# One recurrence stage, four engines: squares and weight halves change engine, and a GELU polynomial is written in one operation fewer

## The chip, the core and the metric

The kernel runs on one core of one Trainium2 chip, in one launch. Its engines are TensorE (PE, matrix products), VectorE (DVE), ScalarE (ACT), GpSimd (POOL) and SyncE (SP, which issues all the DMAs here). Each engine takes its own instructions in order, and semaphores order them against each other. The metric is the device time of the launch in microseconds (us), as the median of several runs.

## The reference, cut to what matters

The program is one layer of an encoder on a 1024 x 1024 float32 input: a mixer, and then a gated feed-forward network with a convolution. Half of the mixer is a gated linear recurrence over the sequence in both directions, the other half attention. The change lies in the recurrence, and in one weight load of the attention that falls into the same stretch of time.

```python
r = sigmoid(xh @ w_a + b_a);  i = sigmoid(xh @ w_x + b_x)      # the gates, block by block
log_a = -LRU_C * r * softplus(-lam)
a = exp(log_a)
u = sqrt(-expm1(2.0 * log_a)) * (i * xf)                        # scaled input of the recurrence
h = associative_scan(a * h_before + u)                          # one forward, one backward
y_lru = gelu(lru_g) * (h_forward + h_backward)
```

The GELU is the one with tanh: 0.5 p (1 + tanh(GK (p + 0.044715 p^3))).

## The kernel before, in words

Channels lie on the 128 partitions and the sequence of 1024 positions on the free axis. Products are made with three float32r matmuls each: an operand is split into an upper half (a rounded copy) and a lower half (the rest), by `split(hi, lo, src, hi_on, lo_on)` at L60 to L67. The upper half is a copy on ACT (L62), DVE (L64) or POOL (L66); the lower half is a subtraction on DVE or POOL (both L67).

The recurrence has 512 channels, so four blocks j = 0 to 3 of 128 channels. For each block and both directions d: a gate product on PE (`psg`), its tanh on ACT (L487), the decay `a` by Exp on ACT (L203), its square (`square_a`, L210, on POOL), a second function of the same gate by Tanh on ACT (L207), their product on DVE (`decay_mul`, L213), one square root for both directions (`root`, L216, on ACT, with a table load in front of it), the gated input (L490, DVE), its scaling (`scale_in`, L219: direction 0 on DVE, direction 1 on POOL), the scan (L223, DVE), the sum of the directions (L226), and the product with the GELU (L229). The GELU of block j is `gelu_a` (L232 to L234) and `gelu_b` (L237 and L238): a square on ACT, a multiply-add and a product on DVE, a tanh on ACT, a last step on DVE that is also the last reader of the PSUM tile `psG`. PSUM has three large tiles in this stretch, for `psg`, `psG` and `psx` (the input projection of a later block) in turn.

Weights come as float32 by DMA into staging tiles `st` (three of them) and are split into tiles `w` (three of them) or `gwt` (gate weights, one): `load` in the block loop, `load_gates` and `load_kv`. Upper halves of these are on DVE, lower halves on POOL.

Two ways of ordering meet here. In blocks 0 and 1 only PE has an order written by hand; the other engines' instructions are put in order when the program is built, by a planner with its own estimates of time. From `xc3 = conv_a(3)` on (blocks 2 and 3, up to the start of the attention loop) the order in the source is the order on PE, ACT, DVE and POOL. The attention loop after it (t = 2 to 60) is again by hand on PE alone.

Of the kernel before, what the change touches and what calls it, by code (L numbers as in the profile page):

```python
# [12 lines left out]
AF = mybir.ActivationFunctionType  # L13
ALU = mybir.AluOpType
# [3 lines left out]
P = 128  # L18
# [22 lines left out]
def encoder_layer(ctx, tc, x, w_in, wq, wk, wv, gw, wo, wup, wdn, vec, g_mix, g_ffn, g_fin, g_q, g_kv, tab_t, tab_n, out):  # L41
    nc = tc.nc
    act, dve, pool, pe = nc.scalar, nc.vector, nc.gpsimd, nc.tensor
# [16 lines left out]
    def split(hi, lo, src, hi_on="act", lo_on="dve"):  # L60
        if hi_on == "act":
            act.activation(hi, src, AF.Copy)  # L62
        elif hi_on == "dve":
            dve.tensor_copy(hi, src)  # L64
        else:
            pool.tensor_scalar(out=hi, in0=src, scalar1=1.0, scalar2=1.0, op0=ALU.mult, op1=ALU.mult)  # L66
        (dve if lo_on == "dve" else pool).tensor_tensor(out=lo, in0=src, in1=hi.bitcast(F32), op=ALU.subtract)  # L67

    def mm3(ps, l, r, start, stop):
        pe.matmul(ps, l[0], r[0], start=start, stop=False)  # L70
        pe.matmul(ps, l[0], r[1], start=False, stop=False)  # L71
        pe.matmul(ps, l[1], r[0], start=False, stop=stop)  # L72
# [39 lines left out]
    def load_w(col, name, src, hi_on="act", lo_on="pool", st=None):  # L112
        if st is None:
            st = stp.tile([P, NK, P], F32, tag="st", name=name + "s")
        nc.sync.dma_start(out=st, in_=src[:, col:col + P].rearrange("(k p) n -> p k n", p=P))
        w = wp.tile([P, 2, NK, P], F32R, tag="w", name=name)
        split(w[:, 0], w[:, 1], st, hi_on, lo_on)
        return w
# [36 lines left out]
    def bigA(name):  # L155
        return psA.tile([P, 1024], F32, tag="big", bufs=3, name=name)
# [6 lines left out]
    def proj_x(j, wx):  # L163
        psx[j] = bigA(f"psx{j}")
        for hf in range(2):
            project(psx[j], wx, xT, hf)

    def proj_g(j, wg, hf, ks=range(NK)):
        if j not in psG:
            psG[j] = bigA(f"psG{j}")  # L170
        project(psG[j], wg, xT, hf, ks)
# [8 lines left out]
    attn = {}  # L180

    def load_kv():
        st = stp.tile([P, S], F32, tag="st", name="wkvst")
        nc.sync.dma_start(out=st[:, 0:512], in_=wk)
        nc.sync.dma_start(out=st[:, 512:1024], in_=wv)
        attn["kv"] = wp.tile([P, 2, S], F32R, tag="w", name="wkv")
        split(attn["kv"][:, 0], attn["kv"][:, 1], st, "dve", "pool")

    def stage_q(k):
        st = stp.tile([P, S], F32, tag="st", name=f"wqst{k}")  # L190
# [10 lines left out]
    def decay_exp(j, d, a):  # L201
        c = lru_c[:, 2 * j + d:2 * j + d + 1]
        act.activation(a, bc[:, d, :], AF.Exp, scale=c, bias=c)  # L203

    def decay_tanh(j, d):
        c = lru_c[:, 2 * j + d:2 * j + d + 1]
        act.activation(bc[:, d, :], bc[:, d, :], AF.Tanh, scale=c, bias=c)  # L207

    def square_a(a, a2):
        pool.tensor_tensor(out=a2, in0=a, in1=a, op=ALU.mult)  # L210

    def decay_mul(d, a2):
        dve.scalar_tensor_tensor(out=bc[:, d, :], in0=a2, scalar=1.0, in1=bc[:, d, :], op0=ALU.add, op1=ALU.mult)  # L213

    def root():
        act.activation(bc[:, 0:2, :], bc[:, 0:2, :], AF.Sqrt, scale=-0.0625)  # L216

    def scale_in(d, eng=None):
        (eng or (pool if d else dve)).tensor_tensor(out=bc[:, 2 + d, :], in0=bc[:, 2 + d, :], in1=bc[:, d, :], op=ALU.mult)  # L219
# [9 lines left out]
        eng.tensor_tensor(out=y_lru[:, j, :], in0=bc[:, 2, :], in1=t1, op=ALU.mult)  # L229

    def gelu_a(t1, p):
        act.activation(t1, p, AF.Square)  # L232
        dve.tensor_scalar(out=t1, in0=t1, scalar1=0.044715, scalar2=1.0, op0=ALU.mult, op1=ALU.add)
        dve.tensor_tensor(out=t1, in0=p, in1=t1, op=ALU.mult)  # L234

    def gelu_b(t1, p):
        act.activation(t1, t1, AF.Tanh, scale=GK)  # L237
# [15 lines left out]
    if True:  # L253
# [207 lines left out]
        if True:  # L461
            def conv_a(j):
                p = psx[j]
                xc = lp.tile([P, S], F32, tag=f"xc{j % 2}", name=f"xc{j}")
                cw = lambda t: vv[:, V_CW + 4 * j + t:V_CW + 4 * j + t + 1]
                act.activation(xc, p, AF.Identity, scale=cw(2), bias=vv[:, V_CB + j:V_CB + j + 1])
                dve.scalar_tensor_tensor(out=xc[:, 2:], in0=p[:, :-2], scalar=cw(0), in1=xc[:, 2:], op0=ALU.mult, op1=ALU.add)
                dve.scalar_tensor_tensor(out=xc[:, 1:], in0=p[:, :-1], scalar=cw(1), in1=xc[:, 1:], op0=ALU.mult, op1=ALU.add)
                dve.scalar_tensor_tensor(out=xc[:, :-1], in0=p[:, 1:], scalar=cw(3), in1=xc[:, :-1], op0=ALU.mult, op1=ALU.add)
                return xc  # L470

            def conv_b(j, xc):
                xch = lp.tile([P, 2, S], F32R, tag="xch", name=f"xch{j}")
                split(xch[:, 0], xch[:, 1], xc, "dve", "dve")
                return xc, xch

            def conv(j):
                return conv_b(j, conv_a(j))

            def gate(j, d, g):  # L480
                gwt, xch = got[f"g{j}"], cv[j][1]
                psg = bigA(f"psg{j}{d}{g}")
                b = 2 * d + g
                for hf in range(2):
                    mm3(psg[:, ts(hf, 512)], (gwt[:, 0, b, :], gwt[:, 1, b, :]),
                        (xch[:, 0, ts(hf, 512)], xch[:, 1, ts(hf, 512)]), True, True)
                act.activation(bc[:, 2 * g + d, :], psg, AF.Tanh, scale=0.5, bias=gb_h[:, 4 * j + b:4 * j + b + 1])  # L487

            def gated(j, d):
                dve.scalar_tensor_tensor(out=bc[:, 2 + d, :], in0=bc[:, 2 + d, :], scalar=1.0, in1=cv[j][0], op0=ALU.add, op1=ALU.mult)  # L490

            def a_tiles(j):
                return [lp2.tile([P, S], F32, tag="a", bufs=2, name=f"a{j}{d}") for d in range(2)]

            def a2_tile(j, d):
                return lp.tile([P, S], F32, tag="a2", name=f"a2{j}{d}")

            def t1_tile(j):
                return (lp2 if j % 2 else lp).tile([P, S], F32, tag="gt", name=f"t1{j}")

            def load_gates(j, gst=None):
                if gst is None:
                    gst = stp.tile([P, 4, P], F32, tag="st", name=f"gst{j}")
                    nc.sync.dma_start(out=gst, in_=gw[:, j])
                g = lp.tile([P, 2, 4, P], F32R, tag="gw", name=f"gwt{j}")
                split(g[:, 0], g[:, 1], gst, "dve", "pool")
                return g

            got = {"X1": wx1, "G0": wG0, "g0": load_gates(0, gst0)}

            def load(k, j):
                got[f"{k}{j}"] = load_gates(j) if k == "g" else load_w((0 if k == "X" else 512) + j * P, f"w{k}{j}", w_in, "dve")

            cv = {0: conv(0)}
            proj_x(1, got["X1"])
            cv[1] = conv(1)
            order.close()
            order.enter_context(tc.manual_schedule(engines=ORDER_PE))
            for j in range(2):
                load("X", j + 2)  # L520
                aa = a_tiles(j)
                gate(j, 0, 0)
                gate(j, 1, 0)
                for d in range(2):
                    a2 = a2_tile(j, d)
                    decay_exp(j, d, aa[d])
                    square_a(aa[d], a2)
                    decay_tanh(j, d)
                    decay_mul(d, a2)
                proj_g(j, got[f"G{j}"], 0)  # L530
                gate(j, 0, 1)
                gate(j, 1, 1)
                root()
                for d in range(2):
                    gated(j, d)
                    scale_in(d)
                    scan(d, aa[d])
                add_dirs(dve)
                proj_g(j, got[f"G{j}"], 1)
                t1 = t1_tile(j)  # L540
                gelu_a(t1, psG[j])
                gelu_b(t1, psG[j])
                load("g", j + 1)
                load("G", j + 1)
                proj_x(j + 2, got[f"X{j + 2}"])
                if j == 0:
                    cv[2] = conv(2)
                merge(j, t1, dve)
                squares(j, t1)
            load("G", 3)  # L550
# [6 lines left out]
    a2 = a2_tile(2, 0)  # L557
# [10 lines left out]
    a2 = a2_tile(2, 1)  # L568
# [14 lines left out]
    t1 = t1_tile(2)  # L583
# [8 lines left out]
    a2 = [y_lru[:, 3, :], a2_tile(3, 1)]  # L592
# [126 lines left out]
    with ExitStack() as apx2:  # L719
# [112 lines left out]
        for t in range(2, NS - 3):  # L832
# [15 lines left out]
            if t in (54, 56, 58, 60):  # L848
                k = (t - 54) // 2
                if k == 3:  # L850
                    wo345 = ctpool.tile([P, 3, 2, D], F32R, tag="cT", name="wo345")
                    w = wo345[:, 0]
                else:
                    w = wp.tile([P, 2, D], F32R, tag="w", name=f"wo{k}")
# [672 lines left out]
```

## Time and profile before

| | |
|---|---|
| median of 3 runs | 1225.94 us (1224.2 to 1227.89) |
| the profiled execution, time | 1227.5 us |
| its span, first to last instruction | 1225.7 us |
| PE busy | 1167.1 us, 95% of the span |
| DVE busy | 939.6 us, 77% |
| ACT busy | 641.3 us, 52% |
| POOL busy | 260.2 us, 21% |
| mean granted TensorE clock | 0.987 of full speed |

A row of the timeline gives the start of an instruction, its duration, its engine, line and operation, the tiles it writes and reads, and in brackets how long the engine sat idle in front of it and which instruction ended that. A duration runs from an instruction's start on its engine, so it includes any time for which the instruction stood there without moving. The chain of waits is the path of work that ended last, followed back from the end. A table of windows gives busy time in each stretch.

### The profile page before, as it was taken

How to read it: one execution, taken by the hardware profiler on the slowest of the kernel's cores; microseconds unless marked ns; L12 is line 12 of the kernel's file. 1: busy time of each engine (PE TensorE's matmuls, PEld its weight loads, DVE VectorE, ACT ScalarE, POOL GpSimd, SP SyncE). 2: the span in 40 equal slices, each digit the busy share in tenths (PEclk: the TensorE clock that was granted, in tenths of full speed). 3: DMA queues.
4: the chain of work that ended last, by engine and by line, in shares of the span. 5: the costliest groups of instructions: out<-in, count | busy, mean ns of one | idle time of the engine just before them, and what ended most of it. 6: DMA issues, size and time to landing. Idle time of an engine off the chain costs nothing.

```text
span 1225.7 us, 15357 instructions
## 1 busy us (share of the span) xinstructions
PE 1167.1 (95%) x5668; PEld 970.8 (79%) x5668; DVE 939.6 (77%) x1386; ACT 641.3 (52%) x1037; POOL 260.2 (21%) x146
## 2 busy tenths in 40 slices
PE   5999986999999999998899999999999999999997
PEld 5987764788888888776778888888888888888885
DVE  5788789877777765478697778787787877887866
ACT  4735565776767764343554445444444454344453
POOL 2214556621212243254010101101010100000000
PEclk8999998999999999999999999999999999999999
DMA  5311101000000133221233232322333258853333
GB/s 211 96 43 44 43 18 35 18 1 1 1 1 1 35 138 121 68 88 51 60 121 107 77 116 96 120 95 78 112 112 121 80 178 304 288 173 119 96 112 120
DMA packets 93579, 113.38 MB, mean 92 GB/s; under 512 B 5184, under 2 KB 59840, under 8 KB 93504
## 3 DMA queue, kind: packets, MB, share of 16 engines
q1 hardware_dynamic: 93504, 112.40, 27.8%
q8 instruction: 44, 0.72, 0.3%
q14 instruction: 31, 0.25, 0.1%
HBM read 82.76 MB, written 28.57 MB: 91 GB/s over the span
## 4 chain that ended last, share of the span: by engine, by line
PE 81%; DVE 12%; ACT 2%; DMA 2%; issue 2%; SPq 0%; DVEq 0%; POOL 0%; ACTq 0%
PE vl L1076 19%; PE x L1269 9%; PE y L1269 7%; PE gh L1076 5%; PE gl L1076 4%; PE pt L763 4%; PE p L1076 4%; PE av L774 3%; PE av L773 2%; PE sc L70 2%; PE sc L71 2%; PE sc L72 2%; DVE bc L223 1%; PE pso L71 1%; PE pso L72 1%
## 5 line engine op out<-in xcount | busy, mean ns | idle before, releaser
L1076 PE MATMUL vl<-T,w 128*128 128x512 f32 x792 | 195.7, 396 | 2.0 <-ACT gl L1082 1.5
L1076 PEld LDWEIGHTS vl<-T,w 128*128 128x128 f32 x792 | 148.5, 188 | 37.8 <-ACT gl L1082 1.9
L67 POOL TENSOR_TENSOR w<-rg,w 128x1024 fp32r<-128x1024 f32 x21 | 52.0, 2475 | 363.8 <-ACT w L62 227.6
L749 DVE TENSOR_REDUCE nm<-sc 128x1 f32<-128x1024 f32 x64 | 78.1, 1221 | 29.9 <-PE sc L72 29.6
L62 ACT ACTIVATE ptb<-pt 128x512 fp32r<-128x512 f32 x128 | 70.2, 596 | 58.3 <-PE pt L763 57.1
L67 DVE TENSOR_TENSOR ptb<-pt,ptb 128x512 fp32r<-128x512 f32 x128 | 83.0, 680 | 7.0 <-ACT ptb L62 7.0
L756 ACT ACTIVATE pr<-sc,nm 128x1024 f32<-128x1024 f32 x64 | 71.7, 1120 | 2.6 <-DVE nm L749 2.6
L763 PE MATMUL pt<-ident,pr 128*128 128x128 f32 x512 | 67.7, 274 | 3.3 <-DVE ptb L67 3.3
L763 PEld LDWEIGHTS pt<-ident,pr 128*128 128x128 f32 x512 | 59.3, 140 | 14.1 <-DVE ptb L67 5.3
L1076 PE MATMUL gh<-B,w 128*128 128x512 f32 x264 | 64.3, 392 | 1.4 <-DVE T L67 1.4
L773 PE MATMUL av<-ptb,vt 128*128 128x256 f32 x256 | 64.9, 292 | 0.0
L1173 ACT ACTIVATE c<-gh,vv 128x512 f32<-128x512 f32 x22 | 17.1, 778 | 89.1 <-DVE gh L1079 89.1
L774 PE MATMUL av<-ptb,vt 128*128 128x256 f32 x256 | 62.6, 283 | 0.0
L1076 PE MATMUL p<-T,w 128*128 128x512 f32 x252 | 62.5, 397 | 0.0
L1269 PE MATMUL x<-abS 128*128 128x512 f32 x264 | 60.2, 389 | 0.0
L1269 PE MATMUL y<-abS 128*128 128x512 f32 x264 | 60.2, 389 | 0.0
L1076 PEld LDWEIGHTS gh<-B,w 128*128 128x128 f32 x264 | 49.5, 188 | 13.0 <-DVE T L67 1.7
L1076 PE MATMUL vl<-B,w 128*128 128x512 f32 x240 | 58.4, 392 | 0.0
L1269 PEld LDWEIGHTS x<-abS 128*128 128x128 f32 x264 | 49.5, 188 | 10.3
L1269 PEld LDWEIGHTS y<-abS 128*128 128x128 f32 x264 | 49.5, 188 | 10.3
L1076 PE MATMUL gl<-B,w 128*128 128x512 f32 x240 | 57.6, 389 | 0.0
L1076 PEld LDWEIGHTS p<-T,w 128*128 128x128 f32 x252 | 47.4, 188 | 11.4
(647 smaller groups left out, 2972.8 us busy)
## 6 DMA issues: line engine op xcount, KB each, us to landing
rg<-in_wup SPq DMA_DIRECT2D x22, 512.0 KB, 4.2
rv<-in_wup SPq DMA_DIRECT2D x22, 512.0 KB, 3.8
S<-c SPq DMA_DIRECT2D x44, 256.0 KB, 2.6
wr<-in_wdn SPq DMA_DIRECT2D x44, 256.0 KB, 5.0
stS<-S SPq DMA_DIRECT2D x44, 256.0 KB, 2.9
A<-c SPq DMA_DIRECT2D x33, 256.0 KB, 2.1
stA<-A SPq DMA_DIRECT2D x33, 256.0 KB, 4.5
wost<-in_wo SPq DMA_DIRECT2D x8, 512.0 KB, 3.8
```

The lines of the kernel that those rows point to most:

```text
L62: act.activation(hi, src, AF.Copy)
L67: (dve if lo_on == "dve" else pool).tensor_tensor(out=lo, in0=src, in1=hi.bitcast(F32), op=ALU.subtract)
L70: pe.matmul(ps, l[0], r[0], start=start, stop=False)
L71: pe.matmul(ps, l[0], r[1], start=False, stop=False)
L72: pe.matmul(ps, l[1], r[0], start=False, stop=stop)
L749: dve.reduce_max(nm[t], sc[t], axis=AX, negate=True)
L756: act.activation(pr[t], sc[t], AF.Exp, bias=nm[t], accum_out=rowsum[:, h, i:i + 1])
L763: pe.transpose(pt[:, ts(c, P)], pr[t][:, ts(4 * kh + c, P)], ident)
L773: pe.matmul(av[:, 0:256], lv, ptb[buf][:, 0, c, :], start=(c == 0), stop=False)
L774: pe.matmul(av[:, 0:256], lv, ptb[buf][:, 1, c, :], start=False, stop=(c == NT - 1))
L1076: pe.matmul(ps, w[:, l, ko + k, :], b[:, r, k, :], start=a_, stop=z_, skip_group_check=True)
L1269: pe.matmul(ps, ab[:, 0, l, ts(j, P)], ab[:, 1, r, :], start=a_, stop=z_, skip_group_check=True)
```

## The change

Four edits. `square_a` becomes a Square on ACT where it was a product on POOL. `gelu_a` makes its Square with a scale of sqrt(0.044715), so that the factor is inside the square, and the multiply-add and the product that followed on DVE become one `scalar_tensor_tensor`: (t1 + 1) p. The upper halves of the gate weights (`load_gates`, four of 128x512), of the weights that `load` fetches (X2, X3, G1, G2 and G3, 128x1024) and of the key and value weights (`load_kv`, 128x1024) are copied on ACT where DVE did it. The lower halves stay on POOL, and no DMA is changed.

```diff
@@ load_kv
-        split(attn["kv"][:, 0], attn["kv"][:, 1], st, "dve", "pool")
+        split(attn["kv"][:, 0], attn["kv"][:, 1], st, "act", "pool")
@@
     def square_a(a, a2):
-        pool.tensor_tensor(out=a2, in0=a, in1=a, op=ALU.mult)
+        act.activation(a2, a, AF.Square)
@@
     def gelu_a(t1, p):
-        act.activation(t1, p, AF.Square)
-        dve.tensor_scalar(out=t1, in0=t1, scalar1=0.044715, scalar2=1.0, op0=ALU.mult, op1=ALU.add)
-        dve.tensor_tensor(out=t1, in0=p, in1=t1, op=ALU.mult)
+        act.activation(t1, p, AF.Square, scale=math.sqrt(0.044715))
+        dve.scalar_tensor_tensor(out=t1, in0=t1, scalar=1.0, in1=p, op0=ALU.add, op1=ALU.mult)
@@ load_gates
-                split(g[:, 0], g[:, 1], gst, "dve", "pool")
+                split(g[:, 0], g[:, 1], gst, "act", "pool")
@@
             def load(k, j):
-                got[f"{k}{j}"] = load_gates(j) if k == "g" else load_w((0 if k == "X" else 512) + j * P, f"w{k}{j}", w_in, "dve")
+                got[f"{k}{j}"] = load_gates(j) if k == "g" else load_w((0 if k == "X" else 512) + j * P, f"w{k}{j}", w_in, "act")
```

## Rows read from the trace of the kernel before

**Rows 1.** Windows, blocks 1, 2, 3: length, busy PE PEld DVE ACT POOL, clock, DMA.

```profile
122.90:157.40 34.50, 29.51 (x120) 23.49 (x120) 27.61 (x19) 17.70 (x16) 15.43 (x6) 0.95 0.13 38
157.40:192.00 34.60, 28.20 (x113) 22.65 (x114) 29.82 (x20) 23.72 (x22) 20.65 (x8) 0.94 0.16 46
192.00:213.80 21.80, 14.94 (x50) 10.85 (x49) 19.86 (x19) 11.26 (x13) 15.06 (x9) 0.87 0.00 1
```

**Rows 2.** Chain of waits, second half of block 1: start, length, what.

```profile
143.94 0.60 DVE wG L64
144.55 2.20 DVE bc L223
146.75 2.74 DVE t L233
...
151.68 1.11 DVE t L234
```

**Rows 3.** Timeline of PE: where it stood idle in blocks 0 and 1.

```profile
89.57 0.50 PE L71 MATMUL psg<-xch,gwt 128*128 128x512 f32 x1 [0.73 <-DVE xch L67]
...
120.78 0.47 PE L70 MATMUL psg<-xch,gwt 128*128 128x512 f32 x1 [2.28 <-DVE t L238]
...
125.13 0.50 PE L70 MATMUL psG<-xT,wG 128*128 128x512 f32 x1 [2.73 <-ACT bc L487]
```

**Rows 4.** Timeline of POOL: a scaling, two lower halves, a square.

```profile
105.20 3.14 POOL L219 TENSOR_TENSOR bc<-bc 128x1024 f32<-128x1024 f32 x1 [0.19 <-ACT bc L216]
...
122.57 2.35 POOL L67 TENSOR_TENSOR wG<-wG2s,wG 128x1024 fp32r<-128x1024 f32 x1 [8.15 <-DVE wG L64]
...
144.63 4.31 POOL L67 TENSOR_TENSOR wG<-wG3s,wG 128x1024 fp32r<-128x1024 f32 x1 [1.76 <-DVE wG L64]
...
190.93 2.87 POOL L210 TENSOR_TENSOR a<-a 128x1024 f32<-128x1024 f32 x1
```

**Rows 5.** Timeline of DVE: two instructions beside POOL's, and one that reads PSUM.

```profile
106.01 3.42 DVE L219 TENSOR_TENSOR bc<-bc 128x1024 f32<-128x1024 f32 x1
...
119.41 1.22 DVE L238 SCALAR_TENSOR_TENSOR t<-t,psG 128x1024 f32<-128x1024 f32 x1
...
146.67 2.81 DVE L233 TENSOR_SCALAR t<-t 128x1024 f32<-128x1024 f32 x1
```

**Rows 6.** Timeline of ACT: prices of the moved work, and where ACT sat idle.

```profile
56.67 1.07 ACT L62 ACTIVATE wG<-wG0s 128x1024 fp32r<-128x1024 f32 x1
...
99.40 1.12 ACT L487 ACTIVATE bc<-psg,gb_h 128x1024 f32<-128x1024 f32 x1 [1.42 <-PE psg L72]
...
118.32 1.06 ACT L237 ACTIVATE t<-t 128x1024 f32<-128x1024 f32 x1 [9.73 <-DVE t L234]
121.92 1.06 ACT L242 ACTIVATE qs<-y_lru 128x1024 f32<-128x1024 f32 x1 [2.55 <-DVE y_lru L229]
...
133.91 1.12 ACT L487 ACTIVATE bc<-psg,gb_h 128x1024 f32<-128x1024 f32 x1 [2.96 <-PE psg L72]
```

**Rows 7.** Chain of waits, blocks 2 and 3.

```profile
176.68 2.81 DVE wkv L64
...
181.69 2.75 DVE t L233
...
190.38 1.67 DVE y_lru L229
192.05 1.75 DVE wq L64
193.80 6.49 issue
...
203.79 2.76 DVE q L67
...
209.49 2.19 DVE t L233
```

**Rows 8.** The page's groups, attention loop: busy, mean ns, idle before and its releaser.

```profile
L763 PE MATMUL pt<-ident,pr 128*128 128x128 f32 x512 | 67.7, 274 | 3.3 <-DVE ptb L67 3.3
```

## The prediction

> **What bounds the kernel now.** I read the page first: PE is busy for 95% of the span, so a change on other engines can only give back what PE loses somewhere. The table of 40 slices shows where: outside one stretch PE stands at 9 or 8 tenths, and in the recurrence, some 88 to 214 us, it falls to 6 to 8 tenths with a lower clock. The windows of that stretch come next [rows 1]: in block 1 PE works 29.5 of 34.5 us, in block 2 28.2 of 34.6, in block 3 14.9 of 21.8, which leaves 5.0, 6.4 and 6.9 us idle, while DVE works 27.6, 29.8 and 19.9. The granted clock is 0.95, 0.94 and 0.87, which says that in part of each window PE ran at the lower of its two levels (1.2 rather than 2.4 GHz), behind the idle time. Who holds PE up is in its timeline [rows 3]: 2.28 us until DVE's last GELU step (L238) frees a PSUM tile, then 2.73 us until a tanh on ACT frees the next. The chain of waits then names the work in front of L238: nearly all of it is DVE [rows 2, 7]. So DVE sets the pace of the recurrence, and ACT, at 17.7 of 34.5 us, does not.
>
> The reader should also see how DVE and POOL stand in each other's way. POOL's scaling runs from 105.20 for 3.14 us, to 108.34 [rows 4]. DVE's own scaling, begun at 106.01, takes 3.42 us and so ends at 109.43, 1.09 us behind POOL's [rows 5]. L233 does the same: begun at 146.67, it ends at 149.48, just behind POOL's lower half, which began at 144.63 and took 4.31 us to 148.94 [rows 4, 5]. That lower half in turn takes 2.35 us when nothing is beside it [rows 4], so it had waited some 1.96 us for the scan in front of L233 [rows 2]. DVE and POOL take turns, by whole instructions, where both work on SBUF.
>
> **The change part by part.**
>
> *GELU in one operation.* Five pairs L233 and L234 become five single instructions. The new one has a form like L238's, one operand in SBUF and one in PSUM, 1.22 us [rows 5]. In block 1 the chain has 2.74 us for L233 and 1.11 for L234, and the second scan between them [rows 2]. L233's 2.74 us are mostly waiting for POOL, and POOL's lower half doesn't go away: it still has to take its turn of 2.35 us between the two scans. But the new operation, which reads PSUM, can run beside it. So after the change the chain has the 2.35 us of POOL with the GELU step under it, in place of 2.74 + 1.11.
>
> *Upper halves on ACT.* Ten DVE copies go (six of 128x1024, four of 128x512). Between DVE's scaling and the scan of block 1 stands one, 0.60 us of the chain [rows 2]. With the item before: 0.60 + 2.74 + 1.11 - 2.35 = 2.1 us for a block under the planner. Bounds: if POOL takes its turn in front of the first scan, with no GELU step to run under it, 1.0 us; if it finds a place beside other work, 0.60 + 2.74 = 3.3 us. I take 2.1, since that is the order of the timeline as it stands. Blocks 0 and 1 give 2 x 2.1 = 4.2 us. PE's idle time has room for it: 2.28 + 2.73 = 5.0 us per block [rows 3].
>
> *What ACT takes on.* A Square of 1024 costs 1.06 us and a copy 1.07, start to end [rows 6]; back to back nearer 1.0. Two squares stand in each block between the Exp and the root, so 2.0 us. ACT idles 1.42 us in block 0 and 2.96 us in block 1 in front of a gate's tanh [rows 6], so block 1 hides them and block 0 lacks 0.6. Ahead of block 0, DVE is rid of two copies, about 1.0 us by the 0.60 above, and PE waits there 0.73 us for DVE's half of `xch` [rows 3]: I set these two against each other, at nothing. The copies should go where ACT waits 9.73 us for the GELU [rows 6]. If the planner puts a 1024 and a 512 copy in front of a root instead, 1.6 us more are on the path, so 3.6 added against 1.42 or 2.96 idle: at worst 2.2 us in block 0 and 0.7 in block 1. With that cover gone altogether each block would lose 3.6. Squares need no table load of their own: L242 ran right behind a tanh, L232 right behind a root, with none between. No DMA is issued elsewhere, and weights split in a block are used in the next, so POOL's lower halves may come some us later at no cost.
>
> *Squares off POOL.* Eight instructions of 1.9 to 2.9 us. In blocks 0 and 1 DVE's waits for them lie in front of the gate products, off the path, so nothing. In block 3 the second, from 190.93 for 2.87 us [rows 4], holds a DVE copy of 128x128 up that is 1.75 us of the chain, and the merge before it lasted 1.67 us [rows 7] against about 1.2 for such an operation: 1.55 and 0.45 us go.
>
> *Blocks 2 and 3*, in the written order. The copy for the keys and values was 2.81 us of the chain [rows 7], but it too stood waiting for POOL's scaling, and the scan behind it needs the same turn; the new squares and the 512 copy make the root some 0.7 us later. I count nothing of the 2.81. L233 of block 2, 2.75, goes as in block 1, but without a copy in front: 2.75 + 1.11 - 2.35 = 1.5. Then 0.45 and 1.55 as above. The 6.49 us called issue are POOL's, waiting for memory of block 3's last gated product on DVE: they move with DVE. The last half of the GELU loses its L233, 2.19. Against that, POOL's two scalings of block 3 come closer to the split of q, which already waits (2.76 us [rows 7] for a lower half of about 0.7): between 0 and one more scaling, 2.4 us; I take 1.2, half way, as the order of the two is open. Sum 1.5 + 0.45 + 1.55 + 2.19 - 1.2 = 4.5 us, with bounds of 3.3 and 5.7, or 8.0 if the copy's 2.81 gave most of itself after all.
>
> *The rule that speaks against it.* Work moves to ACT that DVE does in 0.60 us of the chain and ACT in 1.07 [rows 2, 6]. The Trainium skill, "ScalarE: Activation LUTs", section Rules for kernel authors, says to put multiplications and additions on VectorE and not on ScalarE. By that rule 8 squares and 6 copies of about 1.0 us and 4 copies of half that, some 16 us, land on the dearer engine, and were it on the path the change would lose; rows 6 show where ACT idles.
>
> **Sum.** 4.2 + 4.5 = 8.7 us. The profiled execution took 1227.5 us, so 1218.8; the median is 1.56 us lower, 1225.94, so 1217.2, say 1217. The attention and the network behind it do the same work, so I pass the gain on whole.
>
> **The rivals.**
>
> *ACT takes the place of DVE.* Squares and copies both stand in front of the roots: blocks 0 and 1 keep 2.1 - 2.2 and 2.1 - 0.7, so 1.3 together, and blocks 2 and 3 the lower 3.3: 4.6 us, 1221.3. For it: ACT takes its instructions in order, and the planner chooses. Against: its long idle stretch is close by.
>
> *The turns dissolve.* POOL's halves find places beside PSUM work in each block (3.3 twice) and blocks 2 and 3 give 5.7: 12.3 us, 1213.6, and the lower clock level may be met less often. For it: POOL loses its squares. Against: its scaling and lower half stay next to the scans.
>
> *No difference.* A copy queued ahead of each root and the lower bound twice, with 2.2 and 0.7 lost: 2 x 1.0 - 2.9 + 3.3 = 2.4 us, 1223.5 (1225.94 less 2.4).
>
> *Slower: the attention loop is put in another order.* DVE, ACT and POOL are ordered there by the planner, from a state that this change shifts. Now PE waits only 3.3 us in 512 transposes for DVE [rows 8], so the order is good. The loop has some 60 steps; the gain of 8.7 is gone once each costs 8.7/60 = 0.15 us more, and at 0.25 us it is 15 us, so 1232.2. Against: PE is the bound there, and its order is by hand.
>
> **How the numbers follow.** Forecast 1217 with 0.60 (of its own from 1214 to 1220), ACT 0.14, turns dissolved 0.13, no difference 0.07, slower 0.06. What a measurement can tell from no change is about 0.3%, 3.7 us, so 1222.3 to 1229.6. The forecast, the turns and ACT's case are faster: 0.87; same 0.07; slower 0.06. The range takes in the turns' case and ACT's with a little room for the bounds: 1211.5 to 1222.5, and leaves out the last two and tails.
>
> **What would show it.** Right: no L233; the chain of each block goes scan, POOL or GELU, scan; PE's wait for L238 falls from 2.28 to about 0.2 in block 0 and the attention begins some 8 to 9 us earlier. ACT as bound: its idle in front of the tanh (1.42, 2.96) is gone and the root starts later behind the gate product than now. Wrong altogether: the recurrence ends earlier, but the stretch of the attention is longer by as much; or a table load in front of a Square.

## The result, and the profile after

The kernel after takes 1216.12 us (median of 4 runs, 1215.61 to 1217.72) where the kernel before took 1225.07 beside it: ratio 0.9923, 95% interval 0.9902 to 0.9943, so 9.0 us faster. 1217 was forecast, with a gain of 8.7. The sum was right; several of its terms were not, and two that were set at nothing turned out as losses. Line numbers from L234 on are one lower after the change (L237 was L238, L486 was L487); L233 is the new GELU step.

The windows of the same stretches as [rows 1], with the same columns (length, then busy PE, PEld, DVE, ACT, POOL, clock, DMA):

```profile
122.90:157.40 34.50, 31.19 (x125) 25.17 (x126) 26.38 (x18) 23.48 (x22) 14.24 (x5) 0.91 0.12 39
157.40:192.00 34.60, 30.95 (x126) 24.55 (x124) 27.94 (x22) 29.23 (x29) 9.47 (x4) 0.94 0.17 46
192.00:213.80 21.80, 19.13 (x76) 14.36 (x77) 19.96 (x20) 13.39 (x20) 16.94 (x10) 0.92 0.00 0
```

In block 1's window PE now idles 3.3 us rather than 5.0, and ACT's busy time has gone from 17.7 to 23.5 us. The rows no longer lie over the same work, since each stage starts earlier; so the rest of this section goes by milestones. The second half of block 1, on DVE and then on POOL (start, length, what; compare [rows 2, 4, 5]):

```profile
138.70 1.21 DVE L219 TENSOR_TENSOR bc<-bc 128x1024 f32<-128x1024 f32 x1
139.95 4.37 DVE L223 TENSOR_TENSOR_SCAN bc<-a,bc 128x1024 f32<-128x1024 f32 x1
144.25 1.19 DVE L233 SCALAR_TENSOR_TENSOR t<-t,psG 128x1024 f32<-128x1024 f32 x1
145.36 3.32 DVE L223 TENSOR_TENSOR_SCAN bc<-a,bc 128x1024 f32<-128x1024 f32 x1
...
150.96 1.23 DVE L229 TENSOR_TENSOR y_lru<-bc,t 128x1024 f32<-128x1024 f32 x1
```

```profile
138.93 3.25 POOL L219 TENSOR_TENSOR bc<-bc 128x1024 f32<-128x1024 f32 x1 [1.23 <-DVE bc L489]
142.13 4.40 POOL L67 TENSOR_TENSOR wG<-wG3s,wG 128x1024 fp32r<-128x1024 f32 x1
```

As forecast, the new step L233 takes 1.19 us while POOL's lower half (142.13 to 146.53) is under way, and the second scan then waits for the rest of that half (3.32 us rather than 2.20). Not forecast: DVE's scaling now begins at 138.70, 0.23 us ahead of POOL's, and takes 1.21 us instead of 3.42; POOL's scaling is met by the first scan, 4.37 us. The Trainium skill ("SBUF — State Buffer", section Who interferes with whom) says that a VectorE instruction with two inputs in SBUF contends with a GpSimd instruction that reads SBUF, and that one with at most one input there, outside the 2-port modes that the page names, does not. The trace agrees on the first: the scans stretch from about 2.3 us to 4.37 and 3.32. It agrees on the second for the step that reads PSUM, which stays at 1.19; the old L233, with one input in SBUF, did wait (2.81 us in [rows 5], 0.68 with nothing beside it in the run of the squares alone), and no run here shows which mode it was in.

The first half of the same block, on ACT:

```profile
120.26 1.19 ACT L465 ACTIVATE xc<-psx,vv 128x1024 f32<-128x1024 f32 x1
121.35 1.04 ACT L62 ACTIVATE wG<-wG2s 128x1024 fp32r<-128x1024 f32 x1
122.30 2.10 ACT L486 ACTIVATE bc<-psg,gb_h 128x1024 f32<-128x1024 f32 x2
...
134.59 0.62 ACT L62 ACTIVATE gwt<-gst 128x512 fp32r<-128x512 f32 x1
135.23 1.28 ACT L216 ACT_TABLE_LOAD   x1
136.53 1.92 ACT L216 ACTIVATE bc<-bc 128x2048 f32<-128x2048 f32 x1
...
152.22 1.06 ACT L244 ACTIVATE t<-y_lru 128x1024 f32<-128x1024 f32 x1 [5.69 <-DVE y_lru L229]
153.19 1.19 ACT L465 ACTIVATE xc<-psx,vv 128x1024 f32<-128x1024 f32 x1
```

Two copies stand on the path: 0.95 us (121.35 to 122.30) between the convolution (L465) and the gate's tanh, and 0.64 us in front of the root and its table load. Neither lies in the long idle stretch for which I had meant them; one more of each block does (X3 at 106.44, G3 at 139.98, both in front of the GELU's tanh). The last two rows show something older: the square of `y_lru` waits 5.69 us for DVE's last product, and the convolution of a later block stands behind it in ACT's queue, with the next block's gate tanh behind that. It stood so before, too (L242 at 121.92 in [rows 6]).

Between 88 and 152 us, in blocks 0 and 1, PE has one wait of over 1 us left, and the matmuls that follow it are at the lower clock level (compare [rows 3]):

```profile
123.45 0.50 PE L70 MATMUL psG<-xT,wG 128*128 128x512 f32 x1 [4.32 <-ACT bc L486]
...
124.11 0.63 PE L72 MATMUL psG<-xT,wG 128*128 128x512 f32 x1
...
128.11 0.39 PE L71 MATMUL psG<-xT,wG 128*128 128x512 f32 x1
```

The wait for DVE's L238 (2.28 us) is gone. The wait for the tanh has grown from 2.73 to 4.32, in part because PE now comes to it earlier: it is 3.47 in the run of the GELU edit alone below and 3.87 without the copies. A matmul of 0.63 us follows the one before it by 0.43, one of 0.39 by 0.23.

Blocks 2 and 3 in the chain of waits (compare [rows 7]):

```profile
173.77 4.38 DVE bc L223
178.14 1.11 DVE t L233
...
186.62 5.28 issue
...
194.67 1.77 DVE q L64
196.46 2.75 DVE q L67
...
202.15 0.59 DVE t L233
...
204.11 1.14 DVE nm L748
```

The last GELU step is 0.59 where L233 had 2.19, `wkv` and `wq` are no pieces of over 1 us any more, and the lower half of q is as long as it was (2.75). Its upper half is longer, 1.76 us in the timeline, where before it was:

```profile
202.73 1.02 DVE L64 CAST q<-qf 128x512 fp32r<-128x512 f32 x1
```

Attention's first reduction, the last row, starts at 204.03 in the timeline; before, it was 213.69. From there to the end of the span it is 1011.9 us, and 1012.0 before: the gain is passed on whole, and all of it is made by 204 us.

### Where the 9.7 us of the two profiled executions lie

I cut the stretch at the start of the convolution on ACT that stands ahead of each block's gates (87.73, 120.26 and 153.19 after; 88.65, 122.89 and 157.40 before; each makes the input of a later block), at the end of the root and at the end of L229. Between that end and the next convolution it is 1.0 us in each block of both.

| piece | forecast gain | measured |
|---|---|---|
| up to the first of these cuts | 0 | 0.9 |
| block 0, convolution to end of root | 0 | -1.05 (16.48 to 17.53) |
| block 0, end of root to end of L229 | 2.1 | 2.75 (16.76 to 14.01) |
| block 1, convolution to end of root | 0 | -1.44 (16.75 to 18.19) |
| block 1, end of root to end of L229 | 2.1 | 3.02 (16.76 to 13.74) |
| blocks 2 and 3 | 4.5 | 5.45 (56.29 to 50.84) |

I put the 0.9 us in front down to the single executions: in all fourteen profiled here the first cut lies between 86.6 and 88.9 us, in no order that follows the edits. In the first 60 us the granted clock was 0.94 in that execution of before, 1.00 in this of after, and 0.94 again in two of the experiments; but two others at 1.00 were as late (88.5 and 88.75 us), so the cause is not shown.

Blocks 2 and 3 in pieces, with the run that leaves out the copies (below) between the two:

| piece | before | GELU and squares | after |
|---|---|---|---|
| third cut to end of block 2's root | 16.73 | 17.61 | 18.52 |
| to end of L229 | 17.92 | 14.46 | 14.44 |
| to the split of q | 10.68 | 8.52 | 8.52 |
| split of q, both halves | 3.82 | 4.54 | 4.54 |
| to attention's first reduction | 7.14 | 4.82 | 4.82 |

### The profile page after: what moved, and what is told of

It reads as the page before. It is cut to its first block, busy times and chain, and to the rows that moved or that the text cites. A ratio compares the mean times of both kernels' runs of the same rounds, so it can differ in the third digit from the quotient of the medians.

```text
span 1215.9 us, 15339 instructions
## 1 busy us (share of the span) xinstructions
PE 1165.4 (96%) x5668; PEld 970.0 (80%) x5668; DVE 925.7 (76%) x1371; ACT 656.4 (54%) x1055; POOL 241.9 (20%) x138
## 4 chain that ended last, share of the span: by engine, by line
PE 82%; DVE 10%; ACT 3%; DMA 2%; issue 2%; SPq 0%; DVEq 0%; POOL 0%; ACTq 0%
PE vl L1075 19%; PE x L1268 9%; PE y L1268 7%; PE gh L1075 5%; PE gl L1075 4%; PE pt L762 4%; PE p L1075 4%; PE av L773 3%; PE av L772 3%; PE sc L70 2%; PE sc L71 2%; PE sc L72 2%; DVE bc L223 2%; PE pso L71 1%; PE pso L72 1%
## 5 line engine op out<-in xcount | busy, mean ns | idle before, releaser
L1172 ACT ACTIVATE c<-gh,vv 128x512 f32<-128x512 f32 x22 | 17.1, 778 | 89.1 <-DVE gh L1078 89.1
```

## The experiments

All kernels below were compared with the kernel before on the same chip. Theory of the prediction: DVE's waits for POOL and its own instructions set the pace, and ACT has room. Main rival: ACT takes DVE's place. The first six runs do one part of the change alone, or leave one out.

**The GELU edit alone** (before, with this):

```diff
-        act.activation(t1, p, AF.Square)
-        dve.tensor_scalar(out=t1, in0=t1, scalar1=0.044715, scalar2=1.0, op0=ALU.mult, op1=ALU.add)
-        dve.tensor_tensor(out=t1, in0=p, in1=t1, op=ALU.mult)
+        act.activation(t1, p, AF.Square, scale=math.sqrt(0.044715))
+        dve.scalar_tensor_tensor(out=t1, in0=t1, scalar=1.0, in1=p, op0=ALU.add, op1=ALU.mult)
```

> The kernel before with the GELU edit alone. By the theory of the turns (DVE and POOL alternate by whole instructions, and only what stands on the chain counts) each of blocks 0 to 2 gives 2.74 + 1.11 - 2.35 = 1.5 us and the last half of block 3 2.19 us: 6.7 us in all, some 1218.5 us against 1225. By the rival that DVE's busy time is what counts, the whole 11.1 us of L233 go, some 1214 us. By the rival that POOL's squares are the cause of the gain, under 2 us.

Measured: 0.9934 (0.992 to 0.9947), 1219.64 us, as the turns had it; the 1214 us of DVE's busy time and the 2 us of POOL's squares lie outside the interval. Block 0 of its timeline shows the step as the prediction drew it, in before's order:

```profile
105.16 3.42 DVE L219 TENSOR_TENSOR bc<-bc 128x1024 f32<-128x1024 f32 x1
...
109.10 2.28 DVE L223 TENSOR_TENSOR_SCAN bc<-a,bc 128x1024 f32<-128x1024 f32 x1
111.30 1.19 DVE L233 SCALAR_TENSOR_TENSOR t<-t,psG 128x1024 f32<-128x1024 f32 x1
112.41 3.32 DVE L223 TENSOR_TENSOR_SCAN bc<-a,bc 128x1024 f32<-128x1024 f32 x1
```

**The squares alone** (before, with this):

```diff
-        pool.tensor_tensor(out=a2, in0=a, in1=a, op=ALU.mult)
+        act.activation(a2, a, AF.Square)
```

> The kernel before with the decay squares alone on ACT. Theory of the turns: nothing in blocks 0 and 1, or up to 0.6 us lost there, and 1.55 + 0.45 us gained in block 3: about 1.5 us gained, 1223.5 us. Rival, POOL's squares are the cause: 18 us of POOL's work leave the stretch in which POOL and DVE alternate, and most of the gain of 9 us shows here, under 1219 us. Rival, DVE's busy time: nothing.

Measured: 0.9986 (0.9973 to 0.9999), 1225.91 us, near the 1.5 us of the turns and far from POOL's squares as the cause.

**The copies alone** (before, with "act" for "dve" in `load_kv`, `load_gates` and `load`):

> The kernel before with the upper weight halves alone on ACT. Theory of the turns: 0.60 us in each of blocks 0 and 1, less what a copy in front of a gate's tanh costs (1.0 us where the planner puts one there, as in block 1 of the changed kernel), and of the 2.81 us of the key and value copy little: between 1 us lost and 2 us gained, 1224 to 1226 us. Rival, DVE's busy time: the ten copies were 9.7 us of it, 1216 to 1219 us.

Measured: 1.0017 (1.0007 to 1.0027), 1228.56 us: slower, by 2.1 us where the turns allowed 1 (the interval reaches down to 0.9), and far from the rival's 1216 to 1219. ACT in its block 1:

```profile
123.08 1.19 ACT L466 ACTIVATE xc<-psx,vv 128x1024 f32<-128x1024 f32 x1
124.17 1.05 ACT L62 ACTIVATE wG<-wG2s 128x1024 fp32r<-128x1024 f32 x1
125.12 2.11 ACT L487 ACTIVATE bc<-psg,gb_h 128x1024 f32<-128x1024 f32 x2
...
138.55 0.63 ACT L62 ACTIVATE gwt<-gst 128x512 fp32r<-128x512 f32 x1
139.19 1.28 ACT L216 ACT_TABLE_LOAD   x1
```

Both copies stand in front of the tanh and of the root here too, so their place is not a matter of the other two parts.

**Each part left out** (after, with that part undone):

> The changed kernel with the ten upper halves back on DVE (GELU and squares changed). Adding up the single edits measured alone (GELU 0.9934, squares 0.9986, copies 1.0017 of the kernel before) gives 0.992 without the copies, about 9.8 us under the kernel before and 1 us or more under the changed kernel. If the copies help once the squares have left POOL (the edits belong together), this is slower than the changed kernel, 0.9935 or above.

Measured: 0.992 (0.9906 to 0.9933), 1216.27 us.

> The changed kernel with the decay squares back on POOL. If the edits add up: 0.9934 and 1.0017 give 0.9951, 6.0 us under the kernel before. If the squares are needed for the copies to pay, since POOL's turns then leave room: 0.997 or above.

Measured: 0.994 (0.9924 to 0.9956), 1219.27 us.

> The changed kernel with the GELU polynomial back in two operations (squares and copies changed). If the edits add up: 0.9986 and 1.0017 give 1.0003, no change from the kernel before. If squares and copies help each other by freeing DVE and POOL together: 0.997 or below.

Measured: 0.999 (0.9979 to 1.0001), 1225.13 us.

The single edits add up within about 0.001 in each of the three. The GELU edit makes the difference. The squares are worth some 2 us in company by the middle values (0.9923 against 0.994, 0.992 against 0.9934), but these intervals overlap; the copies are worth nothing that can be told.

**Copies of G1 to G3 back on DVE** (after, with the copies of X2, X3, the gate weights and the keys and values left on ACT):

```diff
-... else load_w((0 if k == "X" else 512) + j * P, f"w{k}{j}", w_in, "act")
+... else load_w((0 if k == "X" else 512) + j * P, f"w{k}{j}", w_in, "act" if k == "X" else "dve")
```

> The changed kernel with the upper halves of G1, G2 and G3 alone back on DVE. In the changed kernel the copy of G2 (1.04 us) stands on ACT between the convolution and the tanh of block 1's first gate, and PE waits 4.32 us for that tanh where it was 2.73 us. If that place is what the copies cost: 1.0 us faster than the changed kernel, or 1.5 to 2 if PE then also spends less time at the lower clock behind the wait, 0.991. If the copy on DVE costs as much in the chain again (0.60 us and a turn of POOL's): no difference, 0.9923.

Measured: 0.9915 (0.9903 to 0.9928), 1215.54 us, no difference from after that can be told. PE in its block 1:

```profile
122.50 0.50 PE L70 MATMUL psG<-xT,wG 128*128 128x512 f32 x1 [3.04 <-ACT bc L486]
122.84 0.40 PE L71 MATMUL psG<-xT,wG 128*128 128x512 f32 x1
```

Without the copy in front of the tanh the wait is 3.04 us instead of 4.32, and in this execution PE stayed at its upper level behind it.

**The pieces of the stage in all of these.** From one profiled execution each, cut as above (start of the convolution, end of root, end of L229; "low" counts the 512-column matmuls of 0.58 to 0.70 us recorded between block 1's cut and the end of its root; the last column runs from the third cut to attention's first reduction):

| kernel | block 0 to root | root to L229 | block 1 to root | low | root to L229 | blocks 2, 3 |
|---|---|---|---|---|---|---|
| before | 16.48 | 16.76 | 16.75 | 8 | 16.76 | 56.29 |
| GELU alone | 16.53 | 14.96 | 17.72 | 11 | 14.97 | 52.58 |
| squares alone | 16.53 | 17.24 | 17.87 | 12 | 16.93 | 54.46 |
| copies alone | 17.17 | 16.42 | 19.33 | 12 | 16.40 | 55.17 |
| GELU and squares | 16.49 | 15.73 | 17.45 | 10 | 15.45 | 49.95 |
| GELU and copies | 17.15 | 14.69 | 18.73 | 9 | 14.68 | 51.23 |
| squares and copies | 17.53 | 15.80 | 19.10 | 11 | 15.53 | 54.93 |
| after, all three | 17.53 | 14.01 | 18.19 | 7 | 13.74 | 50.84 |
| after, G1 to G3 on DVE | 17.13 | 14.03 | 15.69 | 0 | 14.60 | 49.67 |

In block 0, whose first half has no matmul at the lower level, that half is 16.5 us in every kernel without the copies and 17.1 to 17.5 with them: the gate weights' copy of 0.6 us in front of the root, while the squares cost nothing unless the copies are there. In block 1 the lower level lies over this. If each counted matmul cost 0.20 us (0.43 less 0.23), the four kernels without copies would stand at 15.2 to 15.5 and the four with all copies at 16.8 to 16.9: an estimate of about 1.5 us for copies of 0.95 and 0.64. After with G1 to G3 on DVE stands at 15.7, with the copy of 0.64 alone. By the same estimate the lower level costs 1.6 us in before (8 matmuls) and 1.4 in after (7), so it is not what block 1 lost.

The copies are not a plain loss either. From GELU and squares to all three, the halves behind the root become 1.72 and 1.71 us shorter: with the copies back on DVE, one of them stands between DVE's scaling and the first scan, for 2.88 us in block 0, behind POOL's scaling. Against that the halves in front become 1.04 and 0.74 us longer, and blocks 2 and 3 0.89. What is left, 0.8 us in single executions, is less than the runs can tell from nothing.

**Does the turn of POOL cost what the prediction took?** Theory: DVE loses time only by its turns with POOL, so POOL's scaling taken over by DVE makes the block shorter, though DVE gets 1.2 us of work more. Rival: DVE's busy time decides. After, with the scaling of both directions on DVE in blocks 0 to 2 and that of direction 1 in block 3:

```diff
-        (eng or (pool if d else dve)).tensor_tensor(out=bc[:, 2 + d, :], ...
+        (eng or dve).tensor_tensor(out=bc[:, 2 + d, :], ...
```

> The changed kernel with the scaling of direction 1 on DVE too in all four blocks (in block 3 direction 0 stays on POOL). In the changed kernel each first scan of blocks 0 to 2 lasts 4.37 us, since it stands until POOL's scaling (3.25 us) has had its turn. Theory of the turns: DVE's scaling takes 1.13 us where POOL's turn is 2.2 us, so the first scan starts some 1.1 us earlier in blocks 0 to 2, and block 3 gives 0 to 1.2: 3.3 to 4.5 us faster than the changed kernel, 1212 to 1213 us. Rival, DVE's busy time: four operations of 1.2 us more on DVE, 4.8 us slower than the changed kernel, 1221 us.

Measured: 0.9929 (0.9909 to 0.9948), 1218.52 us. Neither: no difference from after.

```profile
104.60 2.35 DVE L219 TENSOR_TENSOR bc<-bc 128x1024 f32<-128x1024 f32 x2
...
106.39 2.81 POOL L67 TENSOR_TENSOR wX<-wX3s,wX 128x1024 fp32r<-128x1024 f32 x1 [3.93 <-ACT wX L62]
...
106.87 4.49 DVE L223 TENSOR_TENSOR_SCAN bc<-a,bc 128x1024 f32<-128x1024 f32 x1
...
194.56 3.13 DVE L219 TENSOR_TENSOR bc<-bc 128x1024 f32<-128x1024 f32 x1
```

In block 0 POOL's lower half moved up into the place that its scaling had left, and the first scan met that instead: 4.49 us. In block 2 DVE's scalings met the lower half of the keys and values (4.56 us for both), and in block 3 POOL's other work, 3.13 us. In block 1 nothing was met:

```profile
140.47 2.28 DVE L223 TENSOR_TENSOR_SCAN bc<-a,bc 128x1024 f32<-128x1024 f32 x1
140.58 4.37 POOL L67 TENSOR_TENSOR wG<-wG3s,wG 128x1024 fp32r<-128x1024 f32 x1 [4.53 <-ACT wG L62]
```

There the lower half came 0.11 us behind the scan, and the half of the block from the root to L229 took 12.69 us where after has 13.74: the 1.1 us of the theory, in one block of four (0.6 of it lost again in that block's first half, with 9 matmuls at the lower level where after has 7). To take one of POOL's two instructions away gains only where the other does not move up into its place.

**POOL out of the scans' turns** (after, with all scalings, block 3's too, and all those lower halves on DVE):

> The changed kernel with everything that POOL does beside the scans put on DVE: the scaling of direction 1 and, in block 3, of both, and the lower halves of X2, X3, G1 to G3, of the gate weights and of the key and value weights. Theory of the turns: in blocks 0 to 2 the chain has DVE's scaling of 1.13 us where POOL's turn was 2.2, and lower half plus GELU step, 1.13 + 1.11, where POOL's turn was 2.35: 1.1 us a block, 3.4 us faster than the changed kernel, about 0.9895 of the kernel before; the lower halves of the gate weights cost nothing where DVE stands idle. Rival, DVE's busy time: eight operations of 1.2 us for scalings and halves in blocks 0 to 2, three more in block 3 and four halves of 0.6 us are some 14 us more: slower than the changed kernel, 1.00 or above.

Measured: 0.9888 (0.9869 to 0.9906), 1211.19 us.

```profile
104.50 2.37 DVE L219 TENSOR_TENSOR bc<-bc 128x1024 f32<-128x1024 f32 x2
106.78 1.22 DVE L233 SCALAR_TENSOR_TENSOR t<-t,psG 128x1024 f32<-128x1024 f32 x1
107.91 2.29 DVE L223 TENSOR_TENSOR_SCAN bc<-a,bc 128x1024 f32<-128x1024 f32 x1
...
115.80 1.22 DVE L229 TENSOR_TENSOR y_lru<-bc,t 128x1024 f32<-128x1024 f32 x1
...
115.97 1.21 ACT L465 ACTIVATE xc<-psx,vv 128x1024 f32<-128x1024 f32 x1 [6.54 <-PE psx L72]
...
118.03 1.04 ACT L241 ACTIVATE qs<-y_lru 128x1024 f32<-128x1024 f32 x1
```

The number is near to what the turns gave, but it doesn't settle them. From the start of DVE's scaling to the end of L229 block 0 takes 12.5 us (104.50 to 117.02), 13.5 in after (105.79 to 119.27), so the turns are worth 1.0 us there, as in block 1 of the run before. The planner did something else besides: it put the convolution ahead of the square of `y_lru`, where after has it behind, and the two convolutions that follow the first came 4.3 and 8.2 us earlier than in after. Which of the two made the 5 us was open, so the next run took the second by itself.

**The squares of y_lru made late.** After, with those of blocks 0 and 1 made where those of blocks 2 and 3 are, in the attention stage:

```diff
                 merge(j, t1, dve)
-                squares(j, t1)
@@
-        for j in (2, 3):
+        for j in range(4):
             squares(j, bc[:, j, :])
```

> The changed kernel with the sums of squares of y_lru for blocks 0 and 1 made late, with those of blocks 2 and 3. In the changed kernel ACT stands idle for 5.68 us in front of that square in both blocks (it waits for the last product of the block), with the next block's convolution and gate tanh queued behind it, and PE then waits 4.32 and 2.76 us for the tanh. If that queue is what is late now: ACT's convolution starts some 3 us earlier in blocks 1 and 2, PE's idle time there goes, and with it part of the time at the lower clock: 5 to 8 us faster than the changed kernel, 0.986 to 0.988. If DVE's chain is the bound in blocks 1 and 2 all the same (its part of the convolution comes behind the product): under 2 us faster, 0.991.

Measured: 0.9861 (0.9836 to 0.9885), 1206.78 us: as the queue on ACT had it, and not under 2 us. DVE's and POOL's work between scaling and scans is left as in after (14.01 and 13.99 us from root to L229); POOL's sum of the squares moves along. Its timeline:

```profile
116.69 1.21 ACT L465 ACTIVATE xc<-psx,vv 128x1024 f32<-128x1024 f32 x1 [2.79 <-PE psx L72]
...
119.90 0.50 PE L70 MATMUL psG<-xT,wG 128*128 128x512 f32 x1 [0.48 <-ACT bc L486]
```

The convolution waits for its own input from PE and for nothing else, PE's wait for the tanh falls from 4.32 to 0.48 us, and a block takes 28.1 us (116.69 to 144.83) instead of 32.9. Against after it gains 7.6 us by the two ratios and 9.3 by the two medians, nearly as much as the whole change under study or a little more.

**The same, with the copies of G1 to G3 back on DVE:**

> The same with the upper halves of G1 to G3 on DVE, so that no copy stands in front of block 1's gate tanh. By the queue on ACT: up to 1 us faster than with those copies on ACT; by the chain on DVE: up to 0.6 us slower.

Measured: 0.9838 (0.9813 to 0.9862), 1205.18 us, the lowest median of the study; from the kernel before it, it can't be told apart. Its windows of blocks 0 and 1:

```profile
88.40:122.90 34.50, 33.80 (x146) 26.99 (x145) 29.54 (x22) 25.24 (x23) 13.79 (x5) 1.00 0.14 38
122.90:157.40 34.50, 34.50 (x151) 27.88 (x150) 29.85 (x22) 25.79 (x25) 9.23 (x4) 1.00 0.14 39
```

PE is busy for 33.8 and 34.5 of 34.5 us, at a clock of 1.00: it is the bound of blocks 0 and 1.

**And POOL out of the turns of blocks 0 to 2 on top of that.** If PE is the bound, the turns should be worth nothing now.

> The kernel after with all three later edits: squares of y_lru of blocks 0 and 1 made late, upper halves of G1 to G3 on DVE, and in blocks 0 to 2 all scalings and the lower halves of X2, X3, G1 to G3 and of the key and value weights on DVE; block 3 keeps both scalings on POOL. Without this last part the ratio to the kernel before was 0.9838, and PE waited for nothing from 90 to 174 us there. Theory 1 (turns cost time only where PE still waits for DVE): blocks 0 and 1 give nothing more, block 2 at most the 1.0 us by which each block's second half became shorter when POOL was left out; ratio 0.983 to 0.984, 1204.2 to 1205.4 us. Rival 1 (the turns cost their 1.0 us in each block whatever PE does): 3 us more, ratio 0.9814. Rival 2 (busy time on DVE decides: some 1.2 us for a scaling and 1.1 to 1.2 for each lower half, 5 to 7 us in blocks 0 to 2): PE waits for DVE's last GELU step again, ratio 0.988 or more.

Measured: 0.9833 (0.9817 to 0.9849), 1206.15 us: no difference.

```profile
88.40:122.90 34.50, 34.50 (x152) 27.84 (x151) 30.87 (x26) 26.18 (x24) 1.56 (x1) 1.00 0.17 46
122.90:157.40 34.50, 34.50 (x152) 28.11 (x151) 29.05 (x24) 25.84 (x25) 1.90 (x2) 1.00 0.10 31
```

POOL's 13.79 and 9.23 us have gone to 1.56 and 1.90, and the root-to-L229 halves are 1.0 us shorter in each block (14.00 to 13.04, 14.59 to 13.64). Attention's first reduction starts 1.0 us earlier (193.55 to 192.58), not 3, and the span is 0.2 us shorter. So three turns of 1.0 us were worth 1.0 us at most, which this interval can't tell from nothing; the 0.9814 of the first rival lies just outside it, the second's 0.988 far. In these runs a turn costs time only where PE waits for what is queued behind it. That it costs 1.0 us a block in after's order is likely by the two runs with POOL's scalings on DVE, but no run isolates it.

## Why the prediction was right, by its own steps

- **What bounds the kernel.** Half right. The page's slices show less than I read from them: from the second slice up to 153 us PE stands at 9 tenths, and it falls to 8 and 6 only behind that; the windows carry the reading. PE waited for L238, and the GELU edit removed that wait in blocks 0 and 1 (2.28 to none). The second wait, for the tanh on ACT, I read off [rows 3] and put down as room. It was the place where the next loss came in (2.73 to 4.32), and its cause stood in [rows 6]: L242 waits for the block's very end, with the convolution and the tanh queued behind it. Late squares took that wait to 0.48 us and gave 7.6 to 9.3 us.
- **GELU in one operation.** Right in mechanism in blocks 0 and 1, by the rows of the GELU run: one step of 1.19 us beside POOL's lower half, the scan behind it. Priced at 1.5 us a block, it gave 1.8 (16.76 to 14.96). In blocks 2 and 3 it was priced at 1.5 + 2.19 = 3.7, and gave 3.71, but that is luck: in that run the first half of block 2 was 1.1 us longer (16.73 to 17.87), its second half only 0.4 shorter (the sum of the directions now stood 2.73 us beside one of POOL's squares), 2.4 came between L229 and the split of q, where the `wq` copy fell from 1.91 to 0.21 us, 0.3 was lost at the split, and the last half gave 2.3.
- **Chain of blocks 0 and 1, 2.1 us each.** GELU and copies, of which the term was made, gave 2.07 and 2.08, though in another order than I had drawn: there the GELU step ran ahead of both scans. The change gave 2.75 and 3.02. With the squares off POOL, DVE's scaling in block 0 comes 0.2 us ahead of POOL's and takes 1.2 us, in every run where POOL has a scaling to do; with the squares on POOL it takes 3.42 in all four. I had taken that order over from the trace as it stood; the bound of 3.3 held it.
- **ACT's additions, nothing.** This step failed: -1.05 and -1.44 us. The bound named it (copies ahead of the root), and in block 1 the copies' true place was worse, since the planner put one ahead of the tanh as well. Squares without the copies are hidden (16.53 against 16.48 in block 0, where 0.6 was to be lacking); behind the copies they cost 0.4 there (17.17 to 17.53). The copies cost 0.6 to 0.7 in block 0 and by the estimate above about 1.5 in block 1. Copies alone lose 2.1 us (1.0017), which is the rival in which ACT takes DVE's place, for this part of the change. The sign named for it was seen in part: the root came later behind the convolution, and ACT's wait in front of the tanh was gone in block 0, and 1.11 of 2.96 us were left in block 1. No table load stood in front of a Square. The Trainium skill ("ScalarE: Activation LUTs", section Rules for kernel authors) says to put multiplications and additions on VectorE and not on ScalarE. The rule does not speak of GpSimd, from which the squares came: they gained a little (0.9986), and no run puts them on DVE.
- **Squares off POOL, 0.45 + 1.55 = 2.0 us in blocks 2 and 3.** Squares alone gave 1.83 there, by other parts: 1.56 between block 2's root and L229 (0.45 was priced there), 0.74 from L229 to the split of q, less 0.34 at the split and 0.12 in front. The `wq` copy did go from 1.91 to 0.22 us, but ACT's square for the GELU was then late, and DVE waited 0.89 us for it; and the GELU edit alone shortened that copy as well.
- **Copy of the keys and values, nothing; split of q, -1.2.** The copy gave nothing, as counted: root to L229 is 14.46 us with it on DVE and 14.44 with it on ACT. The split of q lost 0.72 us, not 1.2, and in its upper half (1.02 to 1.76); the lower half is unchanged (2.76 to 2.75). What I had set at nothing is the first half of block 2, 1.8 us longer. GELU and squares without the copies gained 6.3 in blocks 2 and 3, the three together 5.45, and the difference of 0.9 us lies in that half alone (17.61 to 18.52, single executions), where the copy of the gate weights (0.62 us) again stands in front of the root.
- **Attention passes the gain on.** Right (1012.0 and 1011.9 us). PE's wait for DVE in the transposes [rows 8] is 3.8 us after the change, so the rival of a reordered loop is out:

```profile
L762 PE MATMUL pt<-ident,pr 128*128 128x128 f32 x512 | 67.7, 274 | 3.8 <-DVE ptb L67 3.8
```

So 8.7 against 9.0 is in part luck: in the profiled executions two terms too small by 0.7 and 0.9, one too small by 1.0 and the 0.9 in front made up for two losses of 1.1 and 1.4 that were set at nothing. Inside blocks 2 and 3 losses of 1.8 and 0.7 us were made up in the same way. That block 1's loss is the copies and not the clock rests on the estimate of 0.20 us a matmul, and no run holds the clock level still.

## What to carry to other kernels

Before pricing work that leaves the busiest engine, look at what the idle engine is waiting for and what stands behind that in its queue: here an instruction with no hurry waited for the block's end, with a convolution and the next block's gate tanh behind it, and moving it was worth about as much as three edits that took work off DVE or POOL. Work given to an engine with idle time is free only if it lands in the idle time; with a planner that is not known beforehand, so price it once at its full length on the path. Where two engines take turns, dropping one of several turns gains only if the next instruction in the queue does not take its place: here it took it in two of the three blocks with a lower half behind the scaling.

## What the runs showed of the hardware that was not expected

- How long PE runs at its lower level behind a wait does not follow the length of that wait: in after 7 matmuls of 0.63 us were recorded behind the 4.32 us of block 1 and 12 behind the 2.76 us of block 2; in the run with G1 to G3 on DVE none behind 3.04 us. So a shorter wait is no assurance of the upper level. At 0.20 us for each matmul, these stretches are 0 to 2.4 us in single executions (the table's column), as much as the 2.1 us between the four runs of after.
- The price of a scan is set by what POOL began just before: 2.28 us with nothing begun, 4.49 where a lower half had begun 0.48 us earlier, and 2.28 again where it began 0.11 us later. The new GELU step beside a lower half stayed at 1.19 to 1.21 us in the runs whose rows of blocks 0 and 1 have the two side by side.
